# An expert stage that gathers and scatters its tokens with one-hot products: fp32 products of two passes, or exact hi and lo parts in one pass

## The chip, the core and the metric

One core of a Trainium2 chip runs the whole program in one launch. The metric is the time of one execution on the device in microseconds (us), the median of several runs. The names of the engines are those of the profile: PE multiplies matrices (PEld is its loading of weights), DVE, ACT and POOL work on rows and elements, SP's queue issues the transfers from device memory to the on-chip buffers.

## What is computed

The reference is one transformer layer of width 1024 over 512 tokens: a token mixer (attention and a recurrent scan), then a mixture of 16 experts, then a second block with a dense feed-forward net (the "ffn"). The change touches the experts alone:

```python
SEQ, D_MODEL, N_EXPERTS, D_EXPERT, CAPACITY_FACTOR = 512, 1024, 16, 1024, 2
# h: layer-normed tokens (512 x 1024), modulated: h * (1 + scale) + shift
# aff = softmax(h @ router_w): 512 x 16
# each expert takes its CAP = 512 * 2 / 16 = 64 best tokens (top-k over the tokens)
# hidden = silu(h[picked] @ w_gate[e]) * (h[picked] @ w_up[e])     64 x 1024
# y      = hidden @ w_down[e]                                      64 x 1024
# out[picked] += aff[picked, e] * y
```

All weights are fp32: three matrices of 4 MiB an expert, 192 MiB in all.

## The kernel before

The token rows lie in four tiles of 128 tokens. `moe_token` normalises one tile into `m.h[i]` (128x1024 fp32, kept for the whole stage), transposes it, and computes the router's scores `aff`. After the fourth tile `moe` ranks the tokens of each expert on DVE: `pos` says for each token and expert which of the 64 places it has, or 0.

The experts are then worked off in pairs, all in one stream:

- **Gather.** DVE compares `pos` with 1 to 64 and so writes the one-hot matrix `P` (128 tokens x 4 tiles x 2 experts x 64 places). For each of 8 blocks of 128 columns, four products (one a token tile) of `m.h[i]` with `P` give 128 columns x 128 places: the picked rows, already transposed (L902). They are fp32, and the trace shows two instructions for each fp32 product: 8 pairs x 8 x 4 x 2 = 512 instructions. ACT and DVE move them into the tiles `XT`, applying scale and shift.
- **`PT`.** The transposed `P`, which the scatter needs (L911, copied by ACT on L912).
- **Gate and up** (L929): for each expert 2 x 8 x 2 products of `XT` with 128x512 of weights into the banks `gu`. The two halves of the columns use two halves of PE's array. `aff` products (L918) pick each place's own weight into `gc`.
- **Hidden row.** ACT computes silu, DVE multiplies in `gc` and the up product (`sil`, L935), PE transposes (L938) and ACT copies to `hidT` (L946).
- **Down** (L952): 16 products with the third matrix into `py`; DVE multiplies with a gain (`gt2`) into the rows of `Y` (L957).
- **Scatter** (L959): after both experts of a pair, 8 products of `PT` with `Y` (128x512, fp32, so 16 instructions) give what is added to the tokens `x`. In the last pair these sums stay in PSUM with x itself (L944), and the layer norm of the second block follows.

The weights come in 192 loads of 1 MiB, each of two blocks of 128 rows, through `raw` (L78) into slots of three rings: rings 0 and 1 with five each, ring 2 with eight. `turns` fixes which ring a load takes. A slot is free when the two blocks that it held have been multiplied, and SP's queue waits for that before it issues the load; behind it all later loads wait too, those of the second block included.

The order on each engine comes from a scheduler that issues by tiles and their readiness in a model of its own, so a change to one kind of product moves others around it.

Of the kernel before, what the change touches and what calls it, by code (L numbers as in the profile page):

```python
# [8 lines left out]
F32 = mybir.dt.float32  # L9
F32R = mybir.dt.float32r  # L10
AF = mybir.ActivationFunctionType
OP = mybir.AluOpType
# [718 lines left out]
def halves(x):  # L731
    return [x[:, :512], x[:, 512:]]
# [17 lines left out]
    K.nc.vector.tensor_scalar(out, x, m, r, op0=OP.subtract, op1=OP.mult)  # L750


def normed(K, out, x, spread):

    nc = K.nc
    m, r = ln_stats(K, halves(x))
    if spread:
        nc.scalar.activation(out, x, AF.Identity, scale=r, bias=ln_bias(K, m, r))
# [22 lines left out]
def moe_start(K, c):  # L781

    nc = K.nc
    m = Moe()
    m.keep = K.pool(c, "e_keep", 1, side="right")
    K.use_ring(c, 5, 5, side="right")
    hp = K.pool(c, "e_h", 1, side="right")
    m.h = [hp.tile([128, D], F32, name=f"h{i}") for i in range(NT)]
    m.aff = m.keep.tile([128, NT, NE], F32, name="aff")
    m.pos = m.keep.tile([128, NT, NE], F32, name="pos")  # L790
    m.cols = m.keep.tile([128, 16], F32, name="ecols")
    m.iota = m.keep.tile([128, CAP], F32, name="iota")
    nc.gpsimd.iota(m.iota, pattern=[[1, CAP]], base=1, channel_multiplier=0, allow_small_or_imprecise_dtypes=True)
    return m
# [29 lines left out]
def moe_token(K, m, pool, i):  # L824

    nc = K.nc
    n = m.h[i]
    normed(K, n, K.x[i], i < NT - 1)
    nT = pool.tile([128, KD, 128], F32, name="nT")
    for g in range(2):  # L830
        p = K.ps()
        for j in range(4):
            k = g * 4 + j
            nc.tensor.transpose(p[:, j * 128:(j + 1) * 128], n[:, k * 128:(k + 1) * 128], K.ident)
        nc.scalar.copy(nT[:, g * 4:g * 4 + 4].rearrange("p a b -> p (a b)"), p)

    p = K.ps()
    for k in range(KD):
        q = k % 4
        nc.tensor.matmul(p[q * 32:(q + 1) * 32, :128], m.rw[:, k], nT[:, k], start=k < 4, stop=k >= 4, tile_position=(0, q * 32))  # L840
    lt = pool.tile([128, 128], F32, name="lt")
    nc.vector.tensor_copy(lt, p[:, :128])
    z = p[:, 256:256 + NE]
    nc.tensor.matmul(z, lt, m.sel, start=True, stop=True)
    a = m.aff[:, i]
    st = K.small1.tile([128, 4], F32, name="est")
    nc.vector.tensor_tensor_reduce(a, z, m.bias, 1.0, 3.0e38, OP.add, OP.min, st[:, 0:1])
    nc.scalar.activation(a, a, AF.Exp, bias=st[:, 0:1], scale=-1.0, accum_out=st[:, 1:2])
    nc.vector.reciprocal(st[:, 2:3], st[:, 1:2])
    nc.vector.tensor_scalar(a, a, st[:, 2:3], None, op0=OP.mult)  # L850


def moe(K, m, wg, wu, wd, mods):

    nc, tc = K.nc, K.tc
    with ExitStack() as c:
        K.use_banks(c, gu=2, tr=2, rt=1, py=1, sc=2)
        xp = K.pool(c, "e_x", KD)
        gp = K.pool(c, "e_p", 2)

        K.rings.append(K.pool(c, "ring2", 8))
        yp = K.pool(c, "e_y", 1)
        gt2 = K.bcast(yp, mods[3], "gt2")
        turns = itertools.cycle([0, 1] * 5 + [2] * 8)
        with ExitStack() as c2:
            rp = K.pool(c2, "e_r", 1)

# [20 lines left out]
        tp = K.pool(c, "e_t", 2)  # L888
        for e0 in range(0, NE, 2):

            XT = [xp.tile([128, 2 * CAP], F32, name="XT") for _ in range(KD)]
            P = gp.tile([128, NT, 2, CAP], F32, name="P")
            Pm = P.rearrange("p i e c -> p i (e c)")
            for i in range(NT):
                nc.vector.tensor_tensor(P[:, i], m.iota[:, None, :].to_broadcast([128, 2, CAP]),
                                        m.pos[:, i, e0:e0 + 2, None].to_broadcast([128, 2, CAP]), op=OP.is_equal)
            for k in range(KD):
                if k % 4 == 0:
                    p4 = K.ps("tr")
                p = p4[:, k % 4 * 128:(k % 4 + 1) * 128]  # L900
                for i in range(NT):
                    nc.tensor.matmul(p, m.h[i][:, k * 128:(k + 1) * 128], Pm[:, i], start=i == 0, stop=i == NT - 1)  # L902
                sh, sc = m.cols[:, k:k + 1], m.cols[:, 8 + k:9 + k]
                if k % 2:
                    nc.scalar.activation(XT[k], p, AF.Identity, scale=sc, bias=sh)
                else:
                    nc.vector.tensor_scalar(XT[k], p, sc, sh, op0=OP.mult, op1=OP.add)
            PT = yp.tile([128, S], F32, name="PT")
            pp = K.ps("rt")
            for i in range(NT):  # L910
                nc.tensor.transpose(pp[:, i * 128:(i + 1) * 128], Pm[:, i], K.ident)  # L911
            nc.scalar.copy(PT, pp)  # L912
            y = yp.tile([128, D], F32, name="Y")
            for e in (e0, e0 + 1):
                p = K.ps("rt")
                for i in range(NT):
                    for h in range(2):
                        nc.tensor.matmul(p[h * 64:(h + 1) * 64, 0:1], P[:, i, e - e0], m.aff[:, i, e:e + 1],  # L918
                                         start=i == 0, stop=i == NT - 1, tile_position=(0, h * 64))
                gc = K.small1.tile([128, 1], F32, name="gc")  # L920
                nc.vector.tensor_copy(gc, p[:, 0:1])
                pg = []
                for w in (wg, wu):
                    p = K.ps("gu")
                    for k0 in range(0, KD, 2):
                        r = K.raw([128, 2, D], dram(w, (e * D + k0 * 128) * D, [[D, 128], [128 * D, 2], [1, D]]), next(turns))
                        for k in range(k0, k0 + 2):
                            for h in range(2):
                                nc.tensor.matmul(p[h * 64:(h + 1) * 64], XT[k][:, (e - e0) * CAP:(e - e0 + 1) * CAP],  # L929
                                                 r[:, k - k0, h * 512:(h + 1) * 512], start=k == 0, stop=k == KD - 1,  # L930
                                                 tile_position=(0, h * 64))
                    pg.append(p)
                sl = tp.tile([128, 512], F32, name="sil")
                nc.scalar.activation(sl, pg[0], AF.Silu)
                nc.vector.scalar_tensor_tensor(sl, sl, gc, pg[1], op0=OP.mult, op1=OP.mult)  # L935
                ph = K.ps("rt")
                for q in range(4):
                    nc.tensor.transpose(ph[:, q * 128:(q + 1) * 128], sl[:, q * 128:(q + 1) * 128], K.ident)  # L938
                if e == NE - 1:

                    acc = [[K.ps(n) for n in ns] for ns in (("sc", "sc"), ("gu", "gu"), ("tr", "tr"))]
                    for a, x in zip(acc, K.x):
                        for p, xh in zip(a, halves(x)):
                            nc.tensor.matmul(p, K.ident, xh, start=True, stop=False)  # L944
                hT = tp.tile([128, 4, 2, 64], F32, name="hidT")
                nc.scalar.copy(hT.rearrange("p a b c -> p (a b c)"), ph)  # L946
                py = K.ps("py")
                for f0 in range(0, KD, 2):
                    r = K.raw([128, 2, D], dram(wd, (e * D + f0 * 128) * D, [[D, 128], [128 * D, 2], [1, D]]), next(turns))
                    for f in range(f0, f0 + 2):  # L950
                        for h in range(2):
                            nc.tensor.matmul(py[h * 64:(h + 1) * 64], hT[:, f % 4, f // 4], r[:, f - f0, h * 512:(h + 1) * 512],  # L952
                                             start=f == 0, stop=f == KD - 1, tile_position=(0, h * 64))
                ro = slice((e - e0) * 64, (e - e0) * 64 + 64)
                for h in range(2):
                    sl = slice(h * 512, (h + 1) * 512)
                    nc.vector.tensor_tensor(y[ro, sl], py[h * 64:(h + 1) * 64], gt2[ro, sl], op=OP.mult)  # L957
            def scatter(p, i, h, start):
                nc.tensor.matmul(p, PT[:, i * 128:(i + 1) * 128], y[:, h * 512:(h + 1) * 512], start=start, stop=True)  # L959

            if e0 < NE - 2:
                for i in range(NT):
# [895 lines left out]
def first_out(K, F, I, cm, mods):  # L1858

    nc = K.nc  # L1860
    with ExitStack() as c:
# [130 lines left out]
```

## Time and profile before

| | |
|---|---|
| median of 3 runs | 3489.3 us (3488.88 to 3494.43) |
| profiled execution, own time | 3489.0 us |
| its span, first to last instruction | 3487.2 us |
| mean granted clock of PE | 0.95 |
| PE, DVE, ACT, POOL busy | 90%, 61%, 39%, 30% |

The busy shares are means over the whole program, in which the expert stage takes less than a sixth. What counts for a change in that stage is read from windows over it. Times in the trace are microseconds from the start of the span. The mean time of one instruction on PE is longer than the spacing from one to the next, since they overlap.

### The profile page before, as it was taken

The numbers are of one execution on the slowest core, as the hardware profiler recorded it, in microseconds if no ns is written. First come the engines' busy times: TensorE is split into PE (matmuls) and PEld (weight loads), VectorE is DVE, ScalarE is ACT, GpSimd is POOL, SyncE is SP. The second block draws the span as 40 slices with busy tenths as digits, with TensorE's granted clock in tenths as the row PEclk, the third lists the DMA queues.
The fourth block names the chain that finished last, engine by engine and source line by source line (L and its number), as shares of the span: only waits on it lengthen the run. The fifth ranks groups of instructions, "written<-read, shape, count | busy, mean of one in ns | idle before, by whom it ended". The sixth has DMA issues, their size and how long they took to land. (4 is left out here: it accounts for less than half of the span.)

```text
span 3487.2 us, 52482 instructions
## 1 busy us (share of the span) xinstructions
PE 3130.2 (90%) x20683; PEld 2450.0 (70%) x20683; DVE 2141.1 (61%) x3732; ACT 1356.0 (39%) x2630; POOL 1063.5 (30%) x1071
## 2 busy tenths in 40 slices
PE   6989876777999997999999989998999989989998
PEld 4765455653434334998877678987898977779987
DVE  5667984463211116765767666757856776858657
ACT  3446564221000003443456543434433455634433
POOL 3134473040000004342431243424432341233423
PEclk9999987988999998999999999999999999999999
DMA  5335265548999992322332123222322322213222
GB/s 208 112 118 192 99 200 169 198 151 323 400 387 373 376 352 79 111 84 98 104 96 66 39 71 109 85 97 95 100 97 97 98 79 64 67 49 111 84 99 95
DMA packets 284775, 508.53 MB, mean 146 GB/s; under 512 B 30430, under 2 KB 206384, under 8 KB 279408
## 3 DMA queue, kind: packets, MB, share of 16 engines
q1 hardware_dynamic: 267520, 487.35, 39.7%
q10 hardware_dynamic: 16336, 17.13, 1.5%
q8 instruction: 162, 2.65, 0.3%
q0 software_dynamic: 672, 0.70, 0.1%
q14 instruction: 85, 0.70, 0.1%
HBM read 473.66 MB, written 31.47 MB: 145 GB/s over the span
## 5 line engine op out<-in xcount | busy, mean ns | idle before, releaser
L100 DVE TENSOR_TENSOR wl<-raw,wh 128x1024 fp32r<-128x1024 f32 (+2 forms) x346 | 395.0, 1155 | 213.3 <-ACT wh L99 212.7
L105 PE MATMUL ps<-hTh,wh 128*128 128x256 f32 (+1 forms) x1656 | 493.4, 301 | 14.7 <-ACT hTh L238 12.5
L99 ACT CAST wh<-raw 128x1024 fp32r<-128x1024 f32 (+2 forms) x348 | 312.6, 920 | 458.0 <-PE ps L107 163.2
L106 PE MATMUL ps<-hTl,wh 128*128 128x256 f32 (+1 forms) x1656 | 489.2, 297 | 0.5 <-DVE hTl L239 0.5
L107 PE MATMUL ps<-hTh,wl 128*128 128x256 f32 (+1 forms) x1656 | 476.8, 297 | 3.4 <-DVE wl L100 3.3
L105 PEld LDWEIGHTS ps<-hTh,wh 128*128 128x128 f32 x1656 | 320.8, 195 | 27.9 <-ACT hTh L238 14.2
L297 POOL TENSOR_TENSOR tmp<-raw 128x512 f32<-128x512 f32 x176 | 246.4, 1407 | 292.0 <-DMA raw<-in_w_ffn_gate_dram 231.4
L106 PEld LDWEIGHTS ps<-hTl,wh 128*128 128x128 f32 x1656 | 321.2, 194 | 10.3 <-DVE hTl L239 1.7
L106 PE MATMUL ps<-wl,hh 128*128 128x512 f32 x832 | 324.0, 389 | 0.0
L107 PEld LDWEIGHTS ps<-hTh,wl 128*128 128x128 f32 x1656 | 314.5, 194 | 12.6 <-DVE wl L100 5.4
L107 PE MATMUL ps<-wh,hl 128*128 128x512 f32 x832 | 322.4, 389 | 0.0
L105 PE MATMUL ps<-wh,hh 128*128 128x512 f32 x832 | 303.6, 390 | 2.8 <-DVE hl L511 2.8
L115 POOL TENSOR_TENSOR rs_o<-rs_t,mhalf 128x1 f32<-128x1 f32 (+1 forms) x46 | 36.1, 811 | 848.7 <-DVE rs_t L114 847.7
L100 DVE TENSOR_TENSOR wl<-tmp,wh 128x1024 fp32r<-128x1024 f32 x176 | 244.6, 1390 | 56.9 <-ACT wh L99 55.8
L297 POOL TENSOR_TENSOR tmp<-raw,tmp 128x512 f32<-128x512 f32 x88 | 122.6, 1393 | 480.0 <-DVE wl L100 480.0
L929 PE MATMUL gu<-raw,XT 128*64 128x512 f32 x1024 | 250.7, 600 | 0.0
L99 ACT CAST wh<-tmp 128x1024 fp32r<-128x1024 f32 x176 | 184.4, 1048 | 92.8 <-POOL tmp L297 63.7
L105 PEld LDWEIGHTS ps<-wh,hh 128*128 128x128 f32 x832 | 155.5, 188 | 34.1 <-DVE hl L511 3.3
L107 PEld LDWEIGHTS ps<-wh,hl 128*128 128x128 f32 x832 | 156.2, 188 | 32.5
L106 PEld LDWEIGHTS ps<-wl,hh 128*128 128x128 f32 x832 | 156.3, 188 | 31.7
L929 PEld LDWEIGHTS gu<-raw,XT 128*64 128x64 f32 x1024 | 70.4, 136 | 133.7 <-issue 125.7
L294 DVE TENSOR_TENSOR u<-u,ps 128x256 f32<-128x256 f32 x308 | 127.6, 414 | 50.6 <-PE ps L107 27.2
(558 smaller groups left out, 7381.6 us busy)
## 6 DMA issues: line engine op xcount, KB each, us to landing
raw<-in_exp_w_gate_dram SPq DMA_DIRECT2D x64, 1024.0 KB
raw<-in_exp_w_up_dram SPq DMA_DIRECT2D x64, 1024.0 KB
raw<-in_exp_w_down_dram SPq DMA_DIRECT2D x64, 1024.0 KB
raw<-in_w_ffn_gate_dram SPq DMA_DIRECT2D x44, 1024.0 KB
raw<-in_w_ffn_up_dram SPq DMA_DIRECT2D x44, 1024.0 KB
raw<-in_w_ffn_down_dram SPq DMA_DIRECT2D x44, 1024.0 KB
raw<-in_w_ada_dram SPq DMA_DIRECT2D x24, 1024.0 KB
raw<-in_w_in_dram SPq DMA_DIRECT2D x36, 512.0 KB
```

What stands on the lines that cost most here:

```text
L99: nc.scalar.copy(h3, src)
L100: (engine or nc.vector).tensor_tensor(l3, src, h3.bitcast(F32), op=OP.subtract)
L105: mm(out, lhs[0], rhs[0], start=start, stop=False)
L106: mm(out, lhs[0], rhs[1], start=False, stop=False)
L107: mm(out, lhs[1], rhs[0], start=False, stop=stop)
L115: self.pow = nc.gpsimd.tensor_tensor(o[:, :n], t[:, :n], self.mhalf[:, :n], op=OP.pow)
L294: self.K.nc.vector.tensor_tensor(o, a, b, op=OP.add)
L297: self.K.nc.gpsimd.tensor_tensor(o, a, b, op=op)
L929: nc.tensor.matmul(p[h * 64:(h + 1) * 64], XT[k][:, (e - e0) * CAP:(e - e0 + 1) * CAP], r[:, k - k0, h * 512:(h + 1) * 512], start=k == 0, ...
```

## The change

The layer-normed tile is no longer kept in fp32. It is written into two passing tiles `m.n` of 128x512 (name `fin`, two for all four token tiles), and two tiles of the type F32R are kept: `mh` is a copy on ACT, `ml` is the rest, subtracted on POOL. The gather multiplies both parts with a `P` of type F32R that holds four experts, 128x256 a product, and is done once in two pairs: 4 quads x 8 x 4 x 2 = 256 products (L909 after). In the same way each pair's y is held as `Yh` (ACT) and `Yl` (DVE), and the scatter multiplies both (L972 after), 128 products. F32R products take one instruction each. `P` has one buffer for two, `XT` has 256 columns, and ring 2 has five slots for eight, so 15 slots in all for 18.

```diff
 def moe_start(K, c):
-    m.h = [hp.tile([128, D], F32, name=f"h{i}") for i in range(NT)]
+    m.hh, m.hl = ([hp.tile([128, D], F32R, name=f"{n}{i}") for i in range(NT)] for n in ("mh", "ml"))
 def moe_token(K, m, pool, i):
-    n = m.h[i]
-    normed(K, n, K.x[i], i < NT - 1)
+    n = m.n
+    mean, r = ln_stats(K, halves(K.x[i]))
+    nm = ln_bias(K, mean, r) if i < NT - 1 else None
+    for o, x in zip(n, halves(K.x[i])):
+        normed(K, o, x, mean, r, nm)
...
+    for h, l, x in zip(halves(m.hh[i]), halves(m.hl[i]), n):
+        nc.scalar.copy(h, x)
+        nc.gpsimd.tensor_tensor(l, x, h.bitcast(F32), op=OP.subtract)
 def moe(K, m, wg, wu, wd, mods):
-        gp = K.pool(c, "e_p", 2)
-        K.rings.append(K.pool(c, "ring2", 8))
+        gp = K.pool(c, "e_p", 1)
+        K.rings.append(K.pool(c, "ring2", 5))
-        turns = itertools.cycle([0, 1] * 5 + [2] * 8)
+        turns = itertools.cycle([0, 1] * 5 + [2] * 5)
...
+            if e0 % 4 == 0:
+                XT = [xp.tile([128, 4 * CAP], F32, name="XT") for _ in range(KD)]
+                P = gp.tile([128, NT, 4, CAP], F32R, name="P")
...
                 for i in range(NT):
-                    nc.tensor.matmul(p, m.h[i][:, k * 128:(k + 1) * 128], Pm[:, i], start=i == 0, stop=i == NT - 1)
+                        for n, h in enumerate((m.hh[i], m.hl[i])):
+                            nc.tensor.matmul(p, h[:, k * 128:(k + 1) * 128], Pm[:, i], start=i + n == 0, stop=i + n == NT)
...
-                    nc.vector.tensor_tensor(y[ro, sl], py[h * 64:(h + 1) * 64], gt2[ro, sl], op=OP.mult)
+                    y = tp.tile([128, 512], F32, name="sil")[ro]
+                    nc.vector.tensor_tensor(y, py[h * 64:(h + 1) * 64], gt2[ro, sl], op=OP.mult)
+                    nc.scalar.copy(yh[ro, sl], y)
+                    nc.vector.tensor_tensor(yl[ro, sl], y, yh[ro, sl].bitcast(F32), op=OP.subtract)
...
             def scatter(p, i, h, start):
-                nc.tensor.matmul(p, PT[:, i * 128:(i + 1) * 128], y[:, h * 512:(h + 1) * 512], start=start, stop=True)
+                for n, t in enumerate((yh, yl)):
+                    nc.tensor.matmul(p, PT[:, i * 128:(i + 1) * 128], t[:, h * 512:(h + 1) * 512], start=start and n == 0, stop=n == 1)
...
+        m.n = [F.fin.tile([128, 512], F32, name="fin") for _ in range(2)]
         moe_router(K, m, tp, I["router_w"], mods)
```

The order of issue on PE around the hidden row of the sixth expert, before (`rt<-ident,sil` are the transposes, `tr` the gather, `py` the down products; a row counts products as written, not instructions):

```order
L929 MATMUL gu<-raw,XT 64x512 x2
L938 MATMUL rt<-ident,sil 128x128 x4
L902 MATMUL tr<-P,h_7403 128x128
L902 MATMUL tr<-P,h_7404 128x128
L902 MATMUL tr<-P,h_7405 128x128
L902 MATMUL tr<-P,h_7406 128x128
L929 MATMUL gu<-raw,XT 64x512 x2
L952 MATMUL py<-raw,hidT 64x512 x16
```

And the same place on PE after the change:

```order
L937 MATMUL gu<-raw,XT 64x512 x8
L926 MATMUL rt<-aff,P 64x1 x8
L946 MATMUL rt<-ident,sil 128x128 x4
L960 MATMUL py<-raw,hidT 64x512 x12
L926 MATMUL rt<-aff,P 64x1
L960 MATMUL py<-raw,hidT 64x512 x4
L926 MATMUL rt<-aff,P 64x1 x7
L937 MATMUL gu<-raw,XT 64x512 x32
L946 MATMUL rt<-ident,sil 128x128 x4
L960 MATMUL py<-raw,hidT 64x512 x8
```

Four gather products and two of gate or up stood between the transposes and the first down product; now the down products follow at once, and `aff` products stand directly ahead of the transposes.

The order on POOL in the token stage, before (L115 is the inverse root of a layer norm or of another norm, one element a row):

```order
L1877 TENSOR_TENSOR raw<-raw 128x1024 x4
L811 MEMSET lt 128x128
L1877 TENSOR_TENSOR raw<-raw 128x1024 x4
L115 TENSOR_TENSOR rs_o<-rs_t,mhalf 128x1 x11
L297 TENSOR_TENSOR tmp<-raw 128x512
L100 TENSOR_TENSOR wl<-raw,wh 128x1024
```

And after, from the first of these inverse roots on:

```order
L115 TENSOR_TENSOR rs_o<-rs_t,mhalf 128x1 x3
L840 TENSOR_TENSOR ml_7407<-fin,mh_7403 128x512 x2
L115 TENSOR_TENSOR rs_o<-rs_t,mhalf 128x1 x2
L840 TENSOR_TENSOR ml_7408<-fin,mh_7404 128x512 x2
L115 TENSOR_TENSOR rs_o<-rs_t,mhalf 128x1 x2
L840 TENSOR_TENSOR ml_7409<-fin,mh_7405 128x512
L115 TENSOR_TENSOR rs_o<-rs_t,mhalf 128x1
L840 TENSOR_TENSOR ml_7409<-fin,mh_7405 128x512
L840 TENSOR_TENSOR ml_7410<-fin,mh_7406 128x512 x2
```

Eight subtracts now stand among the inverse roots.

## Rows read from the trace of the kernel before

**Rows 1.** The page's 40 slices of the span: PE, and transfers in GB/s.

```profile
PE   6989876777999997999999989998999989989998
...
GB/s 208 112 118 192 99 200 169 198 151 323 400 387 373 376 352 79 111 84 98 104 96 66 39 71 109 85 97 95 100 97 97 98 79 64 67 49 111 84 99 95
```

**Rows 2.** Windows: us, busy time (count) of PE, PEld, DVE, ACT, POOL; clock, share, GB/s.

```profile
813.60:1335.80 522.20, 511.21 (x2526) 209.72 (x2526) 92.47 (x181) 39.48 (x73) 0.00 (x0) 0.98 0.93 365
826.00:1300.00 474.00, 464.68 (x2290) 189.40 (x2286) 86.85 (x165) 36.37 (x68) 0.00 (x0) 0.99 0.98 384
```

**Rows 3.** Waits of SP's queue from 820 to 1300: total us, times, longest.

```profile
SPq L78 <- PE gu L929: 295.2, 118, 18.4
SPq L78 <- PE py L952: 109.8, 51, 9.5
```

**Rows 4.** Waits of PE from 820 to 1336: total us, times, longest.

```profile
PE rt L938 <- DVE sil L935: 4.2, 4, 1.2
PE py L952 <- ACT hidT L946: 3.7, 5, 0.7
```

**Rows 5.** A window of 10 us inside the stage, columns as in Rows 2.

```profile
870.00:880.00 10.00, 10.00 (x52) 4.00 (x50) 1.76 (x3) 0.46 (x1) 0.00 (x0) 1.00 1.02 409
```

**Rows 6.** Timeline of the stage's end: start, length, what; the releaser in brackets.

```profile
1330.58 5.37 PE L952 MATMUL py<-raw,hidT 128*64 128x512 f32 x24
...
1345.78 1.04 ACT L99 CAST wh<-raw 128x1024 fp32r<-128x1024 f32 x1
```

**Rows 7.** Groups by line, 813 to 1346: busy us, mean ns of one, idle before.

```profile
L902 PE MATMUL tr<-P,h 128*128 128x128 f32 x512 | 73.3, 289 | 1.6 <-DVE P L895 0.7 <-DVE XT L907 0.6 <-ACT XT L905 0.2
...
L959 PE MATMUL sc<-Y,PT 128*128 128x512 f32 x116 | 60.4, 626 | 1.6 <-DVE Y L957 1.6
...
L957 DVE TENSOR_TENSOR Y<-py,gt 64x512 f32<-64x512 f32 x32 | 22.0, 688 | 144.9 <-PE py L952 133.2 <-PE gu L929 11.3
```

**Rows 8.** PE's timeline from 870 to 892.

```profile
871.09 7.04 PE L952 MATMUL py<-raw,hidT 128*64 128x512 f32 x32
...
881.45 1.98 PE L959 MATMUL sc<-Y,PT 128*128 128x512 f32 x4
883.36 1.94 PE L929 MATMUL gu<-raw,XT 128*64 128x512 f32 x8
885.23 1.60 PE L902 MATMUL tr<-P,h 128*128 128x128 f32 x12
886.77 1.07 PE L929 MATMUL gu<-raw,XT 128*64 128x512 f32 x2
```

**Rows 9.** Two windows of the ffn, columns as in Rows 2.

```profile
1425.00:1435.00 10.00, 10.00 (x84) 9.81 (x83) 9.17 (x14) 5.36 (x8) 4.54 (x4) 1.00 0.30 94
1480.00:1490.00 10.00, 10.00 (x46) 8.29 (x45) 3.17 (x3) 2.11 (x2) 2.59 (x2) 1.00 0.33 105
```

**Rows 10.** PE's timeline from 1094 to 1110.

```profile
1099.88 0.63 PE L918 MATMUL rt<-aff,P 128*64 128x1 f32 x16 [0.73 <-ACT PT L912]
1101.71 1.09 PE L938 MATMUL rt<-ident,sil 128*128 128x128 f32 x4 [1.20 <-DVE sil L935]
1103.53 6.92 PE L952 MATMUL py<-raw,hidT 128*64 128x512 f32 x20 [0.73 <-ACT hidT L946]
```

**Rows 11.** Two more windows of the stage, columns as in Rows 2.

```profile
1100.00:1110.00 10.00, 8.07 (x40) 3.16 (x42) 0.90 (x2) 0.58 (x1) 0.00 (x0) 0.66 0.35 114
1168.00:1178.00 10.00, 8.07 (x38) 3.06 (x40) 0.90 (x2) 0.58 (x1) 0.00 (x0) 0.66 0.43 166
```

**Rows 12.** The page's groups of the whole span: products of the ffn, POOL's subtracts.

```profile
L105 PE MATMUL ps<-hTh,wh 128*128 128x256 f32 (+1 forms) x1656 | 493.4, 301 | 14.7 <-ACT hTh L238 12.5
...
L297 POOL TENSOR_TENSOR tmp<-raw 128x512 f32<-128x512 f32 x176 | 246.4, 1407 | 292.0 <-DMA raw<-in_w_ffn_gate_dram 231.4
...
L106 PE MATMUL ps<-wl,hh 128*128 128x512 f32 x832 | 324.0, 389 | 0.0
```

**Rows 13.** Timeline of SP's queue, 695 to 845: the load that waits longest.

```profile
800.32 23.81 SPq L78 DMA_DIRECT2D raw<-in_exp_w_up_dram  x3
```

More of the change, by code (lines that the diff above doesn't have):

```diff
@@ L750, in ln_rows, with normed @@
     K.nc.vector.tensor_scalar(out, x, m, r, op0=OP.subtract, op1=OP.mult)
-def normed(K, out, x, spread):
+def normed(K, out, x, m, r, nm=None):
     nc = K.nc
-    m, r = ln_stats(K, halves(x))
-    if spread:
-        nc.scalar.activation(out, x, AF.Identity, scale=r, bias=ln_bias(K, m, r))
+    if nm is not None:
+        nc.scalar.activation(out, x, AF.Identity, scale=r, bias=nm)
     else:
@@ L832, in moe_token @@
         for j in range(4):
-            k = g * 4 + j
-            nc.tensor.transpose(p[:, j * 128:(j + 1) * 128], n[:, k * 128:(k + 1) * 128], K.ident)
+            nc.tensor.transpose(p[:, j * 128:(j + 1) * 128], n[g][:, j * 128:(j + 1) * 128], K.ident)
         nc.scalar.copy(nT[:, g * 4:g * 4 + 4].rearrange("p a b -> p (a b)"), p)
+    for h, l, x in zip(halves(m.hh[i]), halves(m.hl[i]), n):
+        nc.scalar.copy(h, x)
+        nc.gpsimd.tensor_tensor(l, x, h.bitcast(F32), op=OP.subtract)
     p = K.ps()
@@ L889, in moe @@
         for e0 in range(0, NE, 2):
[L891 to L900, printed above, removed]
-                for i in range(NT):
-                    nc.tensor.matmul(p, m.h[i][:, k * 128:(k + 1) * 128], Pm[:, i], start=i == 0, stop=i == NT - 1)
[L903 to L907, printed above, removed]
@@ L908, in moe @@
-            PT = yp.tile([128, S], F32, name="PT")
+            if e0 % 4 == 0:
+                XT = [xp.tile([128, 4 * CAP], F32, name="XT") for _ in range(KD)]
+                P = gp.tile([128, NT, 4, CAP], F32R, name="P")
+                Pm = P.rearrange("p i e c -> p i (e c)")
+                for i in range(NT):
+                    nc.vector.tensor_tensor(P[:, i], m.iota[:, None, :].to_broadcast([128, 4, CAP]),
+                                            m.pos[:, i, e0:e0 + 4, None].to_broadcast([128, 4, CAP]), op=OP.is_equal)
+                for k in range(KD):
+                    if k % 2 == 0:
+                        p4 = K.ps("tr")
+                    p = p4[:, k % 2 * 256:(k % 2 + 1) * 256]
+                    for i in range(NT):
+                        for n, h in enumerate((m.hh[i], m.hl[i])):
+                            nc.tensor.matmul(p, h[:, k * 128:(k + 1) * 128], Pm[:, i], start=i + n == 0, stop=i + n == NT)
+                    sh, sc = m.cols[:, k:k + 1], m.cols[:, 8 + k:9 + k]
+                    if k % 2:
+                        nc.scalar.activation(XT[k], p, AF.Identity, scale=sc, bias=sh)
+                    else:
+                        nc.vector.tensor_scalar(XT[k], p, sc, sh, op0=OP.mult, op1=OP.add)
@@ L909, in moe @@
+            e4 = e0 % 4
+            PT = yp.tile([128, S], F32R, name="PT")
             pp = K.ps("rt")
             for i in range(NT):
-                nc.tensor.transpose(pp[:, i * 128:(i + 1) * 128], Pm[:, i], K.ident)
+                nc.tensor.transpose(pp[:, i * 128:(i + 1) * 128], Pm[:, i, e4 * CAP:(e4 + 2) * CAP].bitcast(F32), K.ident)
             nc.scalar.copy(PT, pp)
-            y = yp.tile([128, D], F32, name="Y")
+            yh, yl = (yp.tile([128, D], F32R, name="Y" + n) for n in "hl")
@@ L917, in moe @@
                     for h in range(2):
-                        nc.tensor.matmul(p[h * 64:(h + 1) * 64, 0:1], P[:, i, e - e0], m.aff[:, i, e:e + 1],
+                        nc.tensor.matmul(p[h * 64:(h + 1) * 64, 0:1], P[:, i, e % 4].bitcast(F32), m.aff[:, i, e:e + 1],
                                          start=i == 0, stop=i == NT - 1, tile_position=(0, h * 64))
@@ L928, in moe @@
                             for h in range(2):
-                                nc.tensor.matmul(p[h * 64:(h + 1) * 64], XT[k][:, (e - e0) * CAP:(e - e0 + 1) * CAP],
+                                nc.tensor.matmul(p[h * 64:(h + 1) * 64], XT[k][:, e % 4 * CAP:(e % 4 + 1) * CAP],
                                                  r[:, k - k0, h * 512:(h + 1) * 512], start=k == 0, stop=k == KD - 1,
```

## The prediction

> **What bounds the kernel now.** I read the page's slices first [rows 1]: in the 10th to 15th (a slice is 87.2 us) the transfers run at 323 to 400 GB/s, in the others near 200 and less, and from the 11th on PE is busy nine tenths or more. That is the expert stage; the rest of the kernel is not touched. The windows over it [rows 2] say who sets its pace: from the first gather product (813.6) to the last scatter of the loop (1335.8) PE is busy 511.2 of 522.2 us, DVE and ACT are far below, and the transfers, share 0.98 in the middle, look full too. Two resources look full, so the waits decide. SP's queue, which issues every weight load, waits 295 us for PE's gate and up products and 110 us for the down products [rows 3]: no slot is free, and the loads could come earlier than they do. PE waits about 11 us altogether, 4.2 for the gated row (`sil`) and 3.7 for `hidT` [rows 4], hardly at all for a load. So PE bounds the stage now. The loads follow close behind: with no slot lacking a window moves 409 GB/s [rows 5], the stage's mean is 384 [rows 2]. Call T the end of the last down product; now T = 1330.58 + 5.37 = 1335.95 [rows 6].
>
> **Removed from PE.** Two groups of instructions shrink [rows 7]. Their mean times overlap with those of their neighbours, so I take spacing from start to start at full clock [rows 8].
> Gather: 12 instructions from 885.23 to 886.77, 0.128 us each; 512 x 0.128 = 65.5 us. Afterwards there are 4 quads x 8 blocks x 4 token tiles x 2 parts = 256 single-pass products of 128x256.
> Scatter: 4 from 881.45 to 883.36, 0.478 us each; 112 of 128 stand before T: 53.5 us. Afterwards 112 single-pass products of 128x512.
> Neither kind stands in this stage. The ffn's products have the same shapes and type, and back to back a window of 10 us holds 84 of 128x256 and 46 of 128x512 [rows 9]: 0.119 and 0.217 us. The expert stage also reads weights from many pools, so I round up to 0.12 and 0.22.
> Gather: 65.5 - 30.7 = 34.8 us less. Scatter: 53.5 - 24.6 = 28.9 less. Bounds: nothing gained if a product took its whole mean time (rivals); the windows' figures would give 0.6 more.
>
> **Added waits on PE.** A gather of a pair used to stand between the `sil` transposes and the down products that wait for them. In the order of issue it was absent in 5 of 16 experts; with a gather only in every second pair, the down products follow the transposes at once in 12 of 16 (the sixth expert is shown). PE waits 1.05 us on average for `sil` and 0.74 for `hidT` at such a place (4.2/4 and 3.7/5 [rows 4]): 12 x 1.79 = 21.5 instead of 7.9, so 13.6 us more. Behind these waits PE's own queue stands still, and through it SP, which waits for slots that PE frees. Bounds: 0, if older gate and up products fill in, to 21.5.
> The clock: at 1101.7 the sequence scatter, `aff` products (after 0.73 idle), `sil` transposes (1.20), down products (0.73) ends in 20 down products in 6.92 us [rows 10], where the window's mean granted clock is 0.66 [rows 11], between the levels 1.2 and 2.4 GHz. At full clock 32 take 7.04 [rows 8], so 20 take 4.4: 2.5 us lost. The same happens once more around 1171, and nowhere else in the stage. In the order of issue the `aff` products stand directly ahead of the transposes in these two experts, and after the change in two as well (the sixth is one); I leave this term at 0, with 2.5 us for each place more in the bounds.
>
> **Added work elsewhere.** The `lo` parts: POOL's fp32 subtracts of 128x512 take 1.4 us [rows 12], two for each token tile. Only two `fin` tiles serve all four tiles, so the normalisation of token 3 waits for token 2's second subtract; token 3 leads to the ranking and the first gather. On POOL itself the inverse roots of the second block's layer norms stand between these subtracts in the order, and may come later. I take 1.0 us, bounds 0 and 2.8. ACT's casts lie beside it.
> The y split puts a cast and a subtract behind each multiply. DVE and ACT have room (92 and 39 us of 522 [rows 2]); only scatters wait for it, and PE has gate and up products of the next pair in hand. In each pair the scatter may wait a little more: 2 us in all, bounds 0 and 8 x 1.4 = 11.
> PE's path: 34.8 + 28.9 - 13.6 - 1 - 2 = 47.1 less, T = 1288.8.
>
> **The other floor, the loads.** Three fewer slots, 15 for 18. SP cannot issue past the first 15 loads before a slot comes free: it waits 23.81 us from 800.32 on, until 824.1 [rows 13]; the first gate products set that, and they move by the 1 us above. From about 827 (3 us allowed for that 1 us, the issue and the start, my choice; each us more moves the floor by one) 192 - 15 = 177 loads of 1.0486 MB are left. At 409 GB/s one takes 2.564 us: 453.8 us, to 1280.8. The last load's own products take 4 x 0.44 = 1.8: T cannot be before 1282.6. Before the change this floor was 3 loads or 7.7 us lower, and far from binding.
> The two, 1288.8 and 1282.6, lie 6 us apart, and with 15 slots (38 us of loads) PE will sometimes find a load missing: 3 us for that, between 0 and 10. T = 1292, 44 us before 1335.95.
>
> **Behind T.** From T to the ffn's first cast, 1345.78, there are 9.8 us now [rows 6]. The longer y chain adds a subtract like the multiply it follows, 0.69 us [rows 7], and a cast taken alike (1.4 us); the last 16 scatters save 16 x (0.478 - 0.22) = 4.1. The ffn's first 5 MB, 12.8 us at 409 GB/s, stand behind the last expert loads; landing at 1280.8 + 12.8 = 1293.6 they are in time, in the case of the load floor up to 3 us late. Together 0.
> So 3489.0 (the profiled execution, 0.3 under the median) - 44 = **3445 us**. Own range of this case: 3437 (no interference, waits half covered) to 3455 (all waits, 3 more losses of clock).
>
> **Rivals.**
> 1. *The loads keep the stage's mean.* At 384 GB/s [rows 2] 177 loads take 483 us, T = 827 + 483 + 1.8 = 1312, 24 us gained: 3465. For it: no longer stretch shows more. Against: in that mean SP waited for slots most of the time. 15%.
> 2. *The clock falls at every uncovered place.* Ten more losses of 2.5 us on top of 1292: T = 1317, 3470. For it: each such place has the two idles that stood ahead of the falls, 1.20 and 0.73 [rows 10]. Against: of the five such places before, three kept their clock, those without `aff` products directly ahead. 12%. The Trainium skill, "TensorE: Matmul & The Clock Gate", section "HAM oscillation — how this bites in real kernels", describes a loop in which the same gap returns in every turn and the engine starts slow each time; that is this rival, and by the trace it happened only at some turns.
> 3. *Only the load floor holds*, the waits being filled: T = 1282.6 and the tail as above, 3436. 6%.
> 4. *Slower: the load rate falls.* With PE faster, the loads are the path; it decides at 185.6 MB / (1335.95 - 1.8 - 827 = 507 us) = 366 GB/s. Below that the change costs time, at 358 518 us, T = 1347, about 3500. For it: at 0.98 share the mean is only 384. Against: 409 with the queue filled [rows 5]. 4%. The Trainium skill, "DMA: Bandwidth & Descriptors", section "Where 436 GB/s comes from", gives about 358 GB/s as the limit of a core's memory side for such loads, and would make this the forecast; the trace shows more, so the rule does not hold here and the row decides.
> 5. *Slower: the single-pass products do not stream in this stage.* At their whole mean times, 0.30 and 0.39 us [rows 12], the gather is 76.8 for 65.5, the scatter 43.7 for 53.5, with 16.6 of waits: +18 us, 3507. It decides where a 128x256 product takes 0.22 us. Against: the windows of 84 and 46. 3%.
>
> **How the numbers follow.** Likeliest case 58%, rivals 15, 12, 6, 4 and 3, and 2% for the gain eaten by several. The range from 3433 to 3472 takes in the first three rivals and leaves out the slower ones and the tails, below 2 in 10. Two tenths of a per cent (7 us) is about what a measurement of this kernel can tell from no change: faster 0.92, same 0.02, slower 0.06.
>
> **What would show it.** Right: the gather's window shows some 0.12 us a product, the scatter's 0.22; PE's waits for `sil` and `hidT` sum to about 20 us; SP's waits on PE fall from 405 to under 200 us, and PE waits for loads here and there; the transfers run near 400 GB/s from 827 on; T lies near 1292. Wrong: PE waiting 20 us and more for loads at 384 GB/s (rival 1); granted clock of 0.96 or less in the stage (rival 2); a spacing over 0.15 us for the 128x256 products (rival 5).

## The result, and the profile after

The changed kernel takes 3449.9 us (median of four runs, 3447.05 to 3452.66) against 3489.1 for the kernel before (four runs timed beside it): the ratio is 0.9888, with a 95% interval from 0.9876 to 0.9901. The forecast was 3445, range 3433 to 3472. The profiled execution has a time of 3449.31 and a span of 3447.5 us.

The page's slices of the changed kernel, PE and the transfers, answer to [rows 1]:

```profile
PE   6989876776999986999899989998999988989998
...
GB/s 207 112 114 184 112 187 163 227 160 219 409 409 409 409 398 90 109 98 97 95 83 68 50 62 98 111 86 98 111 86 98 93 87 65 62 43 123 81 98 91
```

The expert stage no longer has slices of 352 to 400 GB/s. Four slices in a row stand at 409, the rate of the best window before [rows 5]. Windows of the changed kernel (columns as in Rows 2: the stage from first gather product to last down product, and two stretches inside):

```profile
819.10:1292.80 473.70, 446.00 (x2270) 179.10 (x2270) 104.42 (x179) 52.27 (x87) 0.00 (x0) 0.99 0.99 395
...
950.00:1050.00 100.00, 94.26 (x506) 40.17 (x505) 22.99 (x41) 12.33 (x21) 0.00 (x0) 1.00 1.02 409
...
1150.00:1250.00 100.00, 92.17 (x456) 35.17 (x452) 23.43 (x38) 10.58 (x18) 0.00 (x0) 1.00 1.02 409
```

The stage lasts 473.7 us, not 522.3; PE is busy 446.0 of them, not 511.4, and idle 27.7, not 11. What it waits for, from 820 to 1300 (total us, times, longest):

```profile
PE rt L946 <- DVE sil L943: 10.6, 11, 1.2
PE py L960 <- ACT hidT L954: 8.1, 12, 0.7
PE gu L937 <- DMA raw<-in_exp_w_up_dram: 5.0, 8, 1.0
...
PE gu L937 <- DMA raw<-in_exp_w_gate_dram: 1.5, 3, 0.6
...
PE sc L972 <- DVE x L980: 0.7, 3, 0.3
```

The first two are the uncovered places, 18.7 us, against 7.9 [rows 4]. The next two are new: PE waits for loads. And yet SP still waits for PE (its queue, 820 to 1300):

```profile
SPq L78 <- PE gu L937: 154.5, 73, 28.9
SPq L78 <- PE py L960: 66.6, 38, 4.3
SPq L78 <- PE sc L972: 45.7, 25, 3.9
```

These and three smaller ones make 311 us, against 413 before (the 405 of [rows 3] and two smaller ones). A wait of SP means that no slot is free; it does not mean that the transfers stand still, and here they don't: the last up load is issued at 1261.05 and its products start at 1280.24, so some seven loads are on their way at once.

The end of the stage, PE's timeline of the changed kernel:

```profile
1272.57 1.94 PE L937 MATMUL gu<-raw,XT 128*64 128x512 f32 x8 [1.04 <-DMA raw<-in_exp_w_up_dram]
...
1277.68 1.94 PE L937 MATMUL gu<-raw,XT 128*64 128x512 f32 x8 [0.26 <-DMA raw<-in_exp_w_up_dram]
1280.24 1.94 PE L937 MATMUL gu<-raw,XT 128*64 128x512 f32 x8 [0.62 <-DMA raw<-in_exp_w_up_dram]
1283.10 0.66 PE L946 MATMUL rt<-ident,sil 128*128 128x128 f32 x4 [0.92 <-DVE sil L943]
...
1287.47 5.37 PE L960 MATMUL py<-raw,hidT 128*64 128x512 f32 x24
```

T is 1287.47 + 5.37 = 1292.84. The last up products start 2.56 us apart (1277.68, 1280.24), which is one load at 409 GB/s: at its end the stage goes at the pace of the loads. The ffn's first cast, in ACT's timeline, comes 10.36 us after T; before it was 9.8 [rows 6]:

```profile
1303.20 1.04 ACT L99 CAST wh<-raw 128x1024 fp32r<-128x1024 f32 x1
```

### The profile page after: what moved, and what is told of

Read it like the earlier page. It is cut to its first block, busy times and chain, and to the rows that moved or that the text cites. A ratio compares the mean times of both kernels' runs of the same rounds, so it can differ in the third digit from the quotient of the medians.

```text
span 3447.5 us, 51984 instructions
## 1 busy us (share of the span) xinstructions
PE 3070.9 (89%) x20427; PEld 2424.0 (70%) x20427; DVE 2159.2 (63%) x3733; ACT 1375.4 (40%) x2657; POOL 1076.0 (31%) x1079
## 5 line engine op out<-in xcount | busy, mean ns | idle before, releaser
L115 POOL TENSOR_TENSOR rs_o<-rs_t,mhalf 128x1 f32<-128x1 f32 (+1 forms) x46 | 36.0, 792 | 785.7 <-DVE rs_t L114 785.5
L937 PE MATMUL gu<-raw,XT 128*64 128x512 f32 x1024 | 237.7, 598 | 7.3 <-DMA raw<-in_exp_w_up_dram 5.0
```

The source lines that it names most:

```text
L115: self.pow = nc.gpsimd.tensor_tensor(o[:, :n], t[:, :n], self.mhalf[:, :n], op=OP.pow)
L937: nc.tensor.matmul(p[h * 64:(h + 1) * 64], XT[k][:, e % 4 * CAP:(e % 4 + 1) * CAP], r[:, k - k0, h * 512:(h + 1) * 512], start=k == 0, sto ...
```

## The experiments

In this table "first gather" and T are read from PE's timeline of each profile, the stage is their difference, and "to T" is the time from the issue of the first load that had to wait for a slot (the 16th with 15 slots) to T. The ratio is to the kernel before, timed beside each run, with its 95% interval.

| run | first gather | T | stage | to T | median | ratio |
|---|---|---|---|---|---|---|
| before | 813.6 | 1335.95 | 522.3 | 512.2 | 3489.1 | |
| after | 819.1 | 1292.84 | 473.7 | 462.5 | 3449.9 | 0.9888 [0.9876, 0.9901] |
| e1 slots 15 | 814.4 | 1335.0 | 520.6 | 509.8 | 3489.1 | 1.0000 [0.9991, 1.0010] |
| e2 gather alone | 812.1 | 1303.4 | 491.3 | 480.3 | 3467.2 | 0.9930 [0.9916, 0.9945] |
| e3 scatter alone | 811.1 | 1297.0 | 486.0 | 475.8 | 3455.8 | 0.9903 [0.9887, 0.9920] |
| e4 after, 128 loads | 817.0 | 1291.1 | 474.1 | | 3443.0 | 0.9866 [0.9851, 0.9880] |
| e5 before, 128 loads | 815.8 | 1328.0 | 512.2 | | 3481.8 | 0.9963 [0.9950, 0.9976] |
| e6 after without lo | 816.4 | 1287.1 | 470.7 | 462.4 | 3441.9 | 0.9854 [0.9839, 0.9869] |
| e7 after, 12 slots | 816.9 | 1302.1 | 485.2 | 473.9 | 3462.7 | 0.9914 [0.9899, 0.9929] |
| e8 after, 4 tiles m.n | 810.6 | 1285.7 | 475.1 | 464.1 | 3444.4 | 0.9866 [0.9845, 0.9888] |
| e9 after again | 817.5 | 1292.5 | 475.0 | 463.8 | 3450.5 | 0.9880 [0.9864, 0.9896] |
| e10 earlier slots | 812.5 | 1286.2 | 473.6 | 464.3 | 3446.4 | 0.9877 [0.9860, 0.9894] |
| e11 lo on DVE | 817.9 | 1292.1 | 474.3 | 462.5 | 3447.6 | 0.9870 [0.9853, 0.9886] |
| e12 scatter's order | 813.8 | 1287.7 | 473.9 | 462.6 | 3443.2 | 0.9861 [0.9846, 0.9876] |

**e1, the slots alone.**

```diff
-        K.rings.append(K.pool(c, "ring2", 8))
+        K.rings.append(K.pool(c, "ring2", 5))
...
-        turns = itertools.cycle([0, 1] * 5 + [2] * 8)
+        turns = itertools.cycle([0, 1] * 5 + [2] * 5)
```

> The kernel before with the third slot set at 5 instead of 8, nothing else. Theory (PE sets the pace before the change): the stage from the first gather product to the last down product stays at 522 us, within 3, and the time at 3489. Rival (slots carry weight already): three loads more after the first release, 3 x 2.56 = 7.7 us, 3497.

The stage takes 520.6 us and the time does not move. Three slots cost nothing while PE sets the pace.

**e2, the gather alone**: the diff of the change without `Yh`, `Yl` and the F32R `PT`.

> The gather part alone (four experts at once, hi and lo rows), with the fp32 scatter of before and 15 slots. Theory: 34.8 us less of products, 13.6 us more of waits for sil and hidT, 1 at the start: about 20 less, 3469. Rival (single-pass 128x256 products do not stream): no gain or a loss, 3489 to 3500. Rival (the waits cost nothing): 34 less, 3455.

The time is 3467, some 22 us less, and the stage 31.0 less. PE's waits in this run, 820 to 1300:

```profile
PE rt L946 <- DVE sil L943: 9.9, 10, 1.2
PE py L960 <- ACT hidT L954: 6.6, 9, 0.7
```

The waits are there (16.5 for 7.9), and the products stream; the rivals of no gain and of free waits are out. The stage gained 11 us more than the 20 expected, though; what that is, e3 shows as well.

**e3, the scatter alone**: the lines on `yh`, `yl`, `PT` and `scatter` of the change's diff, put into the kernel before with 15 slots.

> The scatter part alone (Yh, Yl), with the fp32 gather of each pair and 15 slots. Theory: 28.9 us less of products, 2 more at the y chain: 27 less, 3462; PE's waits stay near those of before, since a gather still stands in each pair. Rival (the scatter's parts wait for the casts): 10 us more of waits for Yl, 3472.

The stage is 36.3 us shorter, the time 3456: more than was costed. PE has no wait for `Yh` or `Yl`, so the rival is out. Part of the surplus is the clock: the granted clock shows no fall in this run's stage and two in that of before [rows 11], some 6 us.

A larger part is the gate and up products, which neither edit touches. They come in fours: two halves of the columns, on two halves of PE's array, each of two instructions. Where the scheduler breaks a run of them inside a four, the half that is left alone takes as long as both. PE's timeline of the kernel before, behind the last line of [rows 8]:

```profile
887.77 1.98 PE L959 MATMUL sc<-Y,PT 128*128 128x512 f32 x4
889.68 1.93 PE L929 MATMUL gu<-raw,XT 128*64 128x512 f32 x6
891.54 0.71 PE L902 MATMUL tr<-P,h 128*128 128x128 f32 x4
```

Six take 1.86 us (889.68 to 891.54), as long as eight (883.36 to 885.23 [rows 8]), and two alone 1.00 (886.77 to 887.77). Counted over the stage, 30 runs are broken so in the kernel before, 11 in e2, 8 in e3 and 5 in the changed kernel. Without idle time and lost clock, all gate and up products together take 242.1 us before, 232.7 in e2, 232.4 in e3 and 232.6 in the changed kernel.

The sum of e2 and e3 would be 31.0 + 36.3 = 67.3 us; the change as a whole has 48.6. Of the 19 us between, 9.6 are this gain, which both runs have and the change has only once; some 3 are the clock in the same way; 6.5 are the waits for loads that the changed kernel has and these two have not.

**e4 and e5, fewer loads**: the same edit in the changed kernel and in the kernel before; the up matrices are left out of the result, since the up products read the gate's slots.

```diff
+                rs = []
                 for w in (wg, wu):
...
-                        r = K.raw([128, 2, D], dram(w, (e * D + k0 * 128) * D, [[D, 128], [128 * D, 2], [1, D]]), next(turns))
+                        if w is wg:
+                            rs.append(K.raw([128, 2, D], dram(w, (e * D + k0 * 128) * D, [[D, 128], [128 * D, 2], [1, D]]), next(turns)))
+                        r = rs[k0 // 2]
```

> The changed kernel, where the up products read the gate's weights, so that 128 of the 192 loads are left and every product stays (the result leaves out the up matrices). Theory A (after the change the loads set the end: from the first release to the end they run at 409 GB/s without a gap): the stage of 473.7 us shrinks to PE's own path, by the 6.5 us of PE's waits for loads and perhaps a few more: 464 to 467, time 3440 to 3443. Theory B (PE alone sets it): no change, 3447 to 3451. Theory C (loads hold PE back widely, also where the wait is put down to others): 15 us and more, under 3435.

> The kernel before, where the up products read the gate's weights (128 of 192 loads left, the up matrices left out of the result). Theory (PE sets the pace before): the stage stays at 522 us within 3 and the time at 3489. Rival (the loads hold PE back before the change too): 10 us and more off.

In the kernel before, my expectation fell: the stage is 10.1 us shorter. A window of e5 shows PE without any idle time or loss of clock:

```profile
820.00:1320.00 500.00, 500.00 (x2473) 202.51 (x2473) 90.91 (x174) 38.96 (x72) 0.00 (x0) 1.00 0.61 234
```

In this run's order gate and up products stand behind every group of transposes: no expert has its down products directly behind them, where 5 have in before. So the 11 us of idle time and some 6 us of lost clock are gone, while 42 broken runs of gate and up products (251.6 us, 9.5 more) take part of it back. With fewer loads the scheduler made another order, and the gain stands in that order and not in a wait that names a load; what the loads themselves would cost in the order of before, the run can't tell. In the changed kernel the edit also brings another order (12 such places become none), but the stage stays at 474.1 us, where theory A had 464 to 467: waits for `sil` go on (7.2 us, up to 1.2 each, ahead of the transposes), and the granted clock falls three times. So e4 shows PE's own path at 474 us in that order; it doesn't isolate the path of the changed kernel's order. Its time of 3443 lies in theory A's range for another reason than the theory's: of the 7 us less, most is behind T, where the ffn's first loads are in early (the first cast comes 0.1 us after T).

**e6, without the lo products**: the result leaves out the lo parts of gather and scatter.

```diff
-                        for n, h in enumerate((m.hh[i], m.hl[i])):
-                            nc.tensor.matmul(p, h[:, k * 128:(k + 1) * 128], Pm[:, i], start=i + n == 0, stop=i + n == NT)
+                        nc.tensor.matmul(p, m.hh[i][:, k * 128:(k + 1) * 128], Pm[:, i], start=i == 0, stop=i == NT - 1)
...
-                for n, t in enumerate((yh, yl)):
-                    nc.tensor.matmul(p, PT[:, i * 128:(i + 1) * 128], t[:, h * 512:(h + 1) * 512], start=start and n == 0, stop=n == 1)
+                nc.tensor.matmul(p, PT[:, i * 128:(i + 1) * 128], yh[:, h * 512:(h + 1) * 512], start=start, stop=True)
```

> The changed kernel without the lo products of gather and scatter: 128 of 256 and 64 of 128 products left, all loads kept (the result leaves out the lo parts). PE has 128 x 0.12 + 56 x 0.22 = 27.7 us less. Theory A (the loads set the end now): the stage stays at 474 us, within 5, and the new idle time of PE goes to waits for loads; time 3444 to 3451. Theory B (PE sets it): 28 us less, 3422.

With some 28 us less of products the stage is 3.0 us shorter, and "to T" is 462.4 for 462.5: the first slot came free 2.9 us earlier after the first gather, and that is all that was gained. Waits for loads take the largest part of the place, 18.6 us (826 to 1284) for 6.5; lost clock (3 us more) and slower gate and up products (6 us more) take most of the rest:

```profile
PE gu L936 <- DMA raw<-in_exp_w_up_dram: 10.0, 18, 0.6
PE gu L936 <- DMA raw<-in_exp_w_gate_dram: 8.6, 14, 0.6
```

This is the run that decides: after the change the loads set the end. Theory B, 28 us less, is out. The landings in the traces agree (a load has landed when the last of its 16 parts has): from the landing of the last up load, which PE waits for, to T it is 12.64 us in the changed kernel, in e6, and in e8 to e12 too.

**e7, twelve slots.**

```diff
-        K.rings.append(K.pool(c, "ring2", 5))
+        K.rings.append(K.pool(c, "ring2", 2))
...
-        turns = itertools.cycle([0, 1] * 5 + [2] * 5)
+        turns = itertools.cycle([0, 1] * 5 + [2] * 2)
```

> The changed kernel with the third slot set at 2, so 12 slots. Theory A: three loads more after the first release, 3 x 2.56 = 7.7 us, 3457; Theory B (PE sets the pace and the loads have room): within 3 us, 3450. Rival C (with fewer slots the stream gets gaps): 15 us and more, with windows of 100 us under 400 GB/s.

The stage is 11.5 us longer, and three loads more are 7.7. The loads count, as in theory A; of the other 3.8 us, 2.6 lie behind the last load, whose landing is 5.0 us ahead of T for 2.4 in the changed kernel. SP issues the last two loads late, at 1286.91 and 1288.63 (1269.36 and 1272.13 in the changed kernel), while the stream runs at 408 GB/s from 840 to 1290.

**e8, four passing tiles**, and **e11, the lo subtracts on DVE**: two tries at the longer way to the first gather.

```diff
-        m.n = [F.fin.tile([128, 512], F32, name="fin") for _ in range(2)]
+        m.n = [F.fin.tile([128, 512], F32, name="fin") for _ in range(4)]
...
-    n = m.n
+    n = m.n[i % 2 * 2:i % 2 * 2 + 2]
```

```diff
-        nc.gpsimd.tensor_tensor(l, x, h.bitcast(F32), op=OP.subtract)
+        nc.vector.tensor_tensor(l, x, h.bitcast(F32), op=OP.subtract)
```

> The changed kernel with four passing tiles m.n instead of two, alternating by token tile. Theory (the shared tiles delay the last token tile, and with it ranking, first gather and first free slot): from the last tile's x to the first gather about 1.5 us less, time 3448 to 3449. Rival (POOL's subtracts or ACT's casts cause the delay): no change in that stretch.

> The changed kernel with the eight lo subtracts of the token stage on DVE instead of POOL. In the changed kernel the way from the first layer norm's inverse root to the first ranking step is 28.5 us, 1.7 more than before. Theory (a DVE step that falls on a POOL subtract takes longer: 1.48 us beside one, 0.53 without): DVE's steps fall back to their short times, and what is left of the 1.7 us is the subtracts' own time on DVE, about 0.7 each for the one or two that stand ahead of the last tile's steps: 26.8 to 28. Rival (the delay comes from the two shared tiles and ACT's casts): 28.5 or more. The time changes by at most 2 us either way.

From the first token tile's inverse root (POOL) to the first ranking step (DVE) it is 26.8 us before, 28.5 after, 28.0 in e8 and 29.3 in e11. So the shared tiles account for 0.5 of the 1.7 us, where 1.5 was expected, and e11 missed its 26.8 to 28; what the rest is, it doesn't settle, since its own subtracts on DVE cost more than they free. The rows do show DVE held up beside POOL. In the changed kernel, `fin` of the last token tile (DVE) and the subtract (POOL) that it falls on:

```profile
795.18 1.26 POOL L840 TENSOR_TENSOR ml<-fin,mh 128x512 fp32r<-128x512 f32 x1
795.25 1.48 DVE L759 TENSOR_SCALAR fin<-x,mv,rs_o 128x512 f32<-128x512 f32 x1 [0.72 <-POOL rs_o L115]
796.85 0.53 DVE L759 TENSOR_SCALAR fin<-x,mv,rs_o 128x512 f32<-128x512 f32 x1
```

And the same two halves in e11, where POOL is idle, 1.00 us together:

```profile
795.74 1.00 DVE L759 TENSOR_SCALAR fin<-x,mv,rs_o 128x512 f32<-128x512 f32 x2 [0.26 <-POOL rs_o L115]
```

**e9, the changed kernel again, and e10, slots free earlier**: e10 has e8's four tiles, and the first expert's gate products are written behind each two gather blocks, not behind all eight.

```diff
...
                     if k % 2:
                         nc.scalar.activation(XT[k], p, AF.Identity, scale=sc, bias=sh)
                     else:
                         nc.vector.tensor_scalar(XT[k], p, sc, sh, op0=OP.mult, op1=OP.add)
+                    if e0 == 0 and k % 2:
+                        if k == 1:
+                            first = K.ps("gu")
+                        gate_up(first, wg, 0, k - 1)
...
```

> The changed kernel once more, as it is, timed in more rounds beside the next one, since its profiled stage is 46.6 us shorter with its start and its way to the ffn, and its median only 39.2. Theory (the rest is drift of unchanged parts between executions): the stage from first gather to last down product is again 474 us within 2, the first new load of the stream to the last down product 462 within 2, and the time anywhere from 3443 to 3452. Rival (something behind the stage is slower after the change): the way from the last down product to the end is again 3 us longer than the mean of the kernels before.

> The changed kernel with four passing tiles m.n, and with the first expert's gate products written directly behind each two gather blocks, so that the first slots come free earlier. Theory A (the loads set the end, counted from the first slot that comes free): that slot is free 1 to 3 us earlier after the first gather, the stage is shorter by as much, 0.5 off ahead of it: 2 to 4 us faster than the changed kernel in the same call. Theory B (PE sets it): stage unchanged within 1, at most 0.6 faster.

e9 has the stage again (475.0) and "to T" 463.8, within the 2 us. From T to the end it takes 2155 us, after 2154.7, before 2151.3; but e1, with the products of before, takes 2156 (3491.4 - 1335.0), so the rival is out, and the profile of before is at the short end. In e10 the first waiting load is issued 9.3 us after the first gather instead of 11.3, and "to T" grows to 464.3, so that the stage is 473.6: nothing gained against the changed kernel's 473.7, 1.4 against e9's 475.0. The loads still set the end (T is 12.64 us behind the landing of the last up load), but theory A's 2 to 4 us did not come: the second waiting load is issued 4.1 us behind the first, for 1.7 in the changed kernel, and from the first of the waiting loads to the last the landings take 2.1 us longer. The median of e10 is 4.1 us under e9's with intervals that overlap, too little to settle anything. No run gave a kernel that is clearly faster than the changed one.

**e12, the scatter's order in the loop.**

```diff
+                    ps = [K.ps("sc") for _ in range(2)]
+                    for n, t in enumerate((yh, yl)):
+                        for h in range(2):
+                            nc.tensor.matmul(ps[h], PT[:, i * 128:(i + 1) * 128], t[:, h * 512:(h + 1) * 512], start=n == 0, stop=n == 1)
                     for h, xh in enumerate(halves(K.x[i])):
-                        p = K.ps("sc")
-                        scatter(p, i, h, True)
+                        p = ps[h]
```

> The changed kernel with the loop's scatter written as Yh, Yh, Yl, Yl for the two halves of a token tile, instead of Yh, Yl, Yh, Yl: neighbours write different banks. From start to start a scatter product in the loop takes 0.32 us in the changed kernel, 0.23 in the last scatter, which is written so. Theory A (two products behind each other into one bank cost the difference): 0.23 to 0.26 us in the loop too, 112 x 0.07 = 8 us less on PE, of which the loads let through little: time 3446 to 3451. Theory B (DVE's additions, 0.68 us for each half, free the two banks too late): spacing stays at 0.30 or more, with PE's waits for x growing.

The run tells nothing on its question: the scheduler issued the products as in the changed kernel, Yh, Yl, Yh, Yl, as PE's timeline of e12 shows:

```profile
889.60 0.40 PE L979 MATMUL sc<-Yl,PT 128*128 128x512 f32 x1
890.18 0.51 PE L979 MATMUL sc<-Yh,PT 128*128 128x512 f32 x1 [0.18 <-DVE x L983]
890.53 0.39 PE L979 MATMUL sc<-Yl,PT 128*128 128x512 f32 x1
890.78 0.50 PE L979 MATMUL sc<-Yh,PT 128*128 128x512 f32 x1
```

Spacing and stage are those of the changed kernel, and so is the kernel in effect; its 3443.2 us beside 3449.9 and 3450.5 says how far medians of four runs lie apart.

## Why the prediction was right

The forecast was 44 us less, by two floors that lie close together; the stage, its start and the way to the ffn's first cast give -48.6 + 1.9 + 0.5 = -46.2, and the medians -39.2. The unchanged parts ahead of and behind the stage were 3.6 and 2.9 us longer in the profile of after than in that of before, which makes the -39.7 between the two profiled executions; over all runs the start of the token stage lies between 766.8 and 774.7. That is drift, not the change.

**PE's products.** The distances from each product's start to PE's next, summed over the stage by a count of the trace, are

```text
                    before   after
gather (tr)          68.3     35.7   512, then 256 products
scatter (sc)         56.7     35.7   112 products
```

The gather gained 32.6 (term: 34.8). Inside a group its products stand 0.12 us apart, as the window of the ffn had said; here from the changed kernel's timeline:

```profile
824.05 0.29 PE L909 MATMUL tr<-P,mh 128*128 128x256 f32 x1
824.18 0.28 PE L909 MATMUL tr<-P,ml 128*128 128x256 f32 x1
824.29 0.28 PE L909 MATMUL tr<-P,mh 128*128 128x256 f32 x1
```

The scatter gained 21.0 (term: 28.9): its products did not keep the 0.22 us of the ffn's window. In the last scatter a product follows after 0.23 us, but in the loop after 0.32 on average. The fence has three stretches: a long run in the loop, a group of four as most of the loop has them, and the last scatter:

```profile
895.47 0.50 PE L972 MATMUL sc<-Yh,PT 128*128 128x512 f32 x1 [0.18 <-DVE x L980]
895.80 0.40 PE L972 MATMUL sc<-Yl,PT 128*128 128x512 f32 x1
896.06 0.50 PE L972 MATMUL sc<-Yh,PT 128*128 128x512 f32 x1
896.40 0.40 PE L972 MATMUL sc<-Yl,PT 128*128 128x512 f32 x1
896.98 0.50 PE L972 MATMUL sc<-Yh,PT 128*128 128x512 f32 x1 [0.19 <-DVE x L980]
...
1004.67 0.50 PE L972 MATMUL sc<-Yh,PT 128*128 128x512 f32 x1
1005.01 0.40 PE L972 MATMUL sc<-Yl,PT 128*128 128x512 f32 x1
1005.25 0.39 PE L972 MATMUL sc<-Yh,PT 128*128 128x512 f32 x1
1005.48 0.40 PE L972 MATMUL sc<-Yl,PT 128*128 128x512 f32 x1
1005.80 1.94 PE L937 MATMUL gu<-raw,XT 128*64 128x512 f32 x8
...
1297.38 0.39 PE L972 MATMUL gu<-Yl,PT 128*128 128x512 f32 x1
1297.61 0.39 PE L972 MATMUL tr<-Yl,PT 128*128 128x512 f32 x1
```

In the one long run, 13 products from 892.67 on, four take 1.51 us (895.47 to 896.98), and DVE's two additions that empty their banks 2 x 0.68 = 1.37; a small wait for DVE stands at every second half. But 84 of the 112 stand in groups of four, mostly between gate and up products; all but three of these groups take 1.03 to 1.13 us (1004.67 to 1005.80), at most 0.28 a product, with no wait for DVE. Whether the distance from 0.23 to 0.28 is two products in a row into one bank is open (e12).

**Gate and up products** were no term of the sum: it took the order's effect on them for nothing. They gave 9.5 us (242.1 to 232.6), since 5 of their runs break inside a four and not 30 (e3).

**Waits.** 12 uncovered places were read from the order, 21.5 us; 11 and 12 waits with 18.7 us came. Beside them no wait for the y chain to speak of; the 2 us for it were not needed.

**The clock.** The term was 0 because two experts before and two after have the `aff` products directly ahead of the transposes. In the changed kernel the clock fell at one of the two, at 901.6 (the third expert), and not at the sixth, with the same idle times (1.20 and 0.68); in e10 it fell at both, and for longer. Windows of the changed kernel (the first row) and of e10 (columns as in Rows 2):

```profile
900.00:910.00 10.00, 9.09 (x36) 3.13 (x38) 0.09 (x1) 0.59 (x1) 0.00 (x0) 0.83 1.02 407
...
893.00:903.00 10.00, 7.46 (x38) 3.07 (x40) 1.61 (x4) 1.17 (x2) 0.00 (x0) 0.66 1.03 408
958.00:968.00 10.00, 8.28 (x26) 2.86 (x28) 0.80 (x2) 0.58 (x1) 0.00 (x0) 0.66 1.02 409
```

Rival 2, a fall at each of the 12, is out: none came at the other uncovered places of these two runs, where PE idles 0.91 us for `sil` or not at all. The `aff` products are no sure sign either way: e3 has one such place and no fall, and e7 one fall (at 1230.9) without them. One short fall for two longer ones is worth some 4 us, which the term of 0 left out.

**The loads.** The rate was right: 409 GB/s in every window from 850 to 1250, so rivals 1 (384) and 4 (366 or less) are out. The limit of some 358 GB/s in the Trainium skill, "DMA: Bandwidth & Descriptors", section "Where 436 GB/s comes from", does not hold in this kernel. What failed is which floor lies higher. I had PE's path at 1288.8 and the loads at 1282.6, with 3 us for their meeting. By e6 the loads set the end. Their floor was too low: from the first issue after a free slot to T it is 462.5 us, while 177 loads at 2.564 are 453.8, and I had added 3 and 1.8. The landings in the trace show where the missing 4 us are. The 16 parts of the first of these loads landed from 834.94 to 835.41, those of the last one from 1285.65 to 1290.48. So the earliest parts came every 2.561 us, as the rate says, but the latest ones, which PE has to wait for, every 2.586: over 176 loads 4.4 us more. Behind the last up load (landed at 1280.20) PE waits for no load any more; the last load lands 2.4 us ahead of T, about 0.6 before its own products' turn.

PE's path, on the other hand, was shorter than summed: 473.7 - 6.5 of waits for loads is 467 us in this order, where the sum says 474. Its two product terms gave 10 us less than forecast, but the gate and up products and the clock, both put at nothing, gave some 14, and the waits and the y chain cost 5 less. That T came out within 1 us, 1292.84 for 1292, is luck: the stage was 473.7 us where the forecast has 477, and it began 4.5 us later than forecast, most of it drift.

**The start** cost 1.9 us, not 1.0; **the tail** 0.5, not 0. [Rows 13] merges three issues: the one that had to wait for a slot is the third, at 823.75. In the changed kernel it came at 830.37, 5.5 of the 6.6 us by the later first gather. Rival 5 (no streaming) is out by e2 and e3. Of the signs that I named, the scatter's 0.22 us was wrong (0.32 on average in the loop), and so was "SP's waits under 200 us", 311 came: SP waits for a slot also where the loads are the bound, as long as each transfer has to queue behind the others.

## What to carry to other kernels

Where two resources are nearly full, sum the path of each on its own, from its own start to its own end; the gains of the parts (31 and 36 us here) don't add up, since a gain that both have counts once, and the nearer floor caps the rest (49). Test which floor binds by taking work from one side only: 28 us of products removed gave 3. With a scheduler, a change to one kind of product moves the cost of another: 9.5 us here came from gate and up products that nobody had edited, and in e5, with fewer loads, another order gave 10. Count what the order does to the products that stay.

## What the runs showed of the hardware that was not expected

- A DVE step of 128x512 took 1.48 us beside a POOL subtract and 0.53 without one.
- Single-pass products of 128x512 stood 0.23 us apart with a new bank each and 0.28 in groups of four where two in a row write one bank; the cause was not separated.
- A run of six gate and up products, two of them without their partners on the other half of the array, took 1.86 us, as long as a run of eight; two alone took 1.00.
- The core moved 409 GB/s over 400 us on end. The 16 parts of a 1 MiB load landed within 0.5 us of each other at the start of that stream and 4.8 us apart at its end.
